# Halving the last row but one between ScalarE and VectorE, and coarser steps in the first two chunks, in a relu row-sum kernel

## The chip, the cores and the metric

The kernel runs on one core of one Trainium2 chip. The metric is the device time of one execution in microseconds (us). Two times appear here. The **time** is what the chip reports for an execution. The **span** is what the profile covers: from the first to the last instruction of the kernel itself. The time is longer, by 1.35 us in the profiled run of the kernel before: it takes in more than the kernel's own instructions.

All runs told of here were with a granted clock of 1.0.

## The reference

```python
# x: 32 x 512 x 1024 float32
relu_x = np.maximum(x, 0)
return np.sum(relu_x, axis=-1).astype(np.float32)
```

There are 16,384 rows of 1024 numbers. On 128 partitions that is 128 rows a partition. 67.1 MB are read and 65 KB are written.

## The kernel before

SyncE issues all transfers on one queue. Seven chunks of 16 rows a partition go through three buffers; then come pieces of 8, 4, 2 and 1 rows, and the last row in three pieces of columns. In the first six chunks ScalarE applies relu to a step of several rows and VectorE sums that step. Later each engine does whole rows alone, with relu and sum in one instruction and an accumulator read of one column (0.19 us on ScalarE, 0.08 on VectorE) after it. The engines and the transfers wait for each other by semaphores: counters that one raises and another waits for.

```python
STEPS = [4, 5, 7]          # rows in each step of chunks 0 to 4
MIXED = [3, 4, 5]          # chunk 5
TAIL = [8, 4, 2, 1]
LAST = [576, 256, 192]     # columns of the pieces of the last row
...
    for c in range(NBIG + 1):
        if c >= NB:
            sp.wait_ge(s_dve, 3 * (c - NB + 1))     # the buffer is free again
        ... sp.dma_start(out=buf[:, c % NB, :, :], ...).then_inc(s_in[c], 16)
...
        for i, n in enumerate(steps):
            t = buf[:, b, r : r + n, :]
            act.activation(t, t, AF.Relu).then_inc(s_act, 1)
            dve.wait_ge(s_act, 3 * c + i + 1)
            dve.tensor_reduce(out=res[...], in_=t, axis=X, op=ALU.add).then_inc(s_dve, 1)
            r += n
...
    for r, n, s in tail:                    # the last of these is row 14, alone
        if n > 1:
            act.wait_ge(s, 16)
        dve.wait_ge(s, 16)
        for i in range(r, r + n):
            f = on_act if (i - r) % 2 else on_dve
            f(buf[:, tb, i, :], res[:, j0 + i : j0 + i + 1])

    n = LAST[2]                             # the last row, in three pieces
    act.wait_ge(s_in[-3], 16)
    on_act(parts[0], last[:, n : n + 1]).then_inc(s_tact, 1)
    dve.wait_ge(s_in[-2], 16)
    on_dve(parts[1], last[:, n + 1 : n + 2]).then_inc(s_tpart, 1)
    dve.wait_ge(s_tpart, 1)
    dve.wait_ge(s_in[-1], 16)
    dve.wait_ge(s_tact, 1)
    on_dve(last[:, :], res[:, J - 1 : J]).then_inc(s_tdve, 1)
```

The sums of the first two pieces are laid behind the third piece, so the last instruction sums 192 numbers and two partial sums.

Of the kernel before, what the change touches and what calls it, by code (L numbers as in the profile page):

```python
# [2 lines left out]

P = 128
D = 1024
BIG = 16
NTWO = 6
NB = 3
REGIONS = [112, 16]
CHUNKS = [(0, 0), (0, 16), (0, 32), (0, 48), (0, 64), (0, 80), (0, 96)]  # L10
STEPS = [4, 5, 7]
MIXED = [3, 4, 5]
TAIL = [8, 4, 2, 1]
LAST = [576, 256, 192]


def bass_relu_sum_kernel(
    nc: bass.Bass,
    x: bass.AP,
    out: bass.AP,  # L20
):







    fp32 = mybir.dt.float32
    ALU = mybir.AluOpType  # L30
    AF = mybir.ActivationFunctionType
    X = mybir.AxisListType.X

    B, S, _ = x.shape
    J = B * S // P
    NBIG = len(CHUNKS)
    assert BIG * NBIG + sum(TAIL) + 1 == J == sum(REGIONS) and sum(LAST) == D

    xr = x.rearrange("b s d -> (b s) d")
    of = out.rearrange("b s -> (b s)")  # L40
    start = [sum(REGIONS[:i]) for i in range(len(REGIONS))]
    xv = [
        xr[P * s : P * (s + n), :].rearrange("(p j) d -> p j d", p=P)
        for s, n in zip(start, REGIONS)
    ]
    ov = [of[P * s : P * (s + n)].rearrange("(p j) -> p j", p=P) for s, n in zip(start, REGIONS)]

    buf = nc.alloc_sbuf_tensor("buf", [P, NB, BIG, D], fp32)
    last = nc.alloc_sbuf_tensor("last", [P, LAST[2] + 2], fp32)
    res = nc.alloc_sbuf_tensor("res", [P, J], fp32)  # L50

    n_in = NBIG + len(TAIL) + len(LAST)
    s_in = [nc.alloc_semaphore(f"s_in{i}") for i in range(n_in)]
    s_act = nc.alloc_semaphore("s_act")
    s_dve = nc.alloc_semaphore("s_dve")
    s_fact = nc.alloc_semaphore("s_fact")
    s_fdve = nc.alloc_semaphore("s_fdve")
    s_tact = nc.alloc_semaphore("s_tact")
    s_tpart = nc.alloc_semaphore("s_tpart")
    s_tdve = nc.alloc_semaphore("s_tdve")  # L60
    s_store = nc.alloc_semaphore("s_store")
    s_out = nc.alloc_semaphore("s_out")

    sp, act, dve = nc.sync, nc.scalar, nc.vector


    tb = NBIG % NB


    code = nc.main_func.blocks[0].instructions  # L70
    arrival = next(
        i
        for i, ins in enumerate(code)
        if ins.engine == mybir.EngineType.SP and type(ins).__name__ == "InstDrain"
    )
    for c in range(NBIG + 1):
        if c >= NB:
            sp.wait_ge(s_dve, 3 * (c - NB + 1))
        if c < NBIG:
            g, j = CHUNKS[c]  # L80
            sp.dma_start(out=buf[:, c % NB, :, :], in_=xv[g][:, j : j + BIG, :]).then_inc(
                s_in[c], 16
            )
        if c == 0:
            code.insert(arrival, code.pop())
    r = 0
    tail = []
    for i, n in enumerate(TAIL):
        sp.dma_start(out=buf[:, tb, r : r + n, :], in_=xv[-1][:, r : r + n, :]).then_inc(  # L89
            s_in[NBIG + i], 16  # L90
        )
        tail.append((r, n, s_in[NBIG + i]))
        r += n
    n0, n1 = LAST[0], LAST[0] + LAST[1]
    parts = [buf[:, tb, r, 0:n0], buf[:, tb, r, n0:n1], last[:, 0 : LAST[2]]]
    for k, (lo, hi) in enumerate([(0, n0), (n0, n1), (n1, D)]):
        sp.dma_start(out=parts[k], in_=xv[-1][:, BIG - 1, lo:hi]).then_inc(
            s_in[NBIG + len(TAIL) + k], 16
        )
    sp.wait_ge(s_fact, 1)  # L100
    sp.wait_ge(s_fdve, 1)
    for g in range(len(REGIONS) - 1):
        sp.dma_start(
            out=ov[g][:, :], in_=res[:, start[g] : start[g] + REGIONS[g]]
        ).then_inc(s_store, 16)


    def on_act(t, acc):
        return act.activation(t, t, AF.Relu, accum_out=acc)  # L109

    def on_dve(t, acc):
        return dve.tensor_scalar(  # L112
            out=t, in0=t, scalar1=0.0, scalar2=None, op0=ALU.max, op1=ALU.add, accum_out=acc
        )

    def row(c, i):
        return buf[:, c % NB, i, :], res[:, c * BIG + i : c * BIG + i + 1]

    for c in range(NTWO):
        b, steps = c % NB, STEPS if c < NTWO - 1 else MIXED  # L120
        act.wait_ge(s_in[c], 16)
        if steps is MIXED:
            dve.wait_ge(s_in[c], 16)
            for i in (BIG - 4, BIG - 3):
                on_dve(*row(c, i))
        r = 0
        for i, n in enumerate(steps):
            t = buf[:, b, r : r + n, :]
            act.activation(t, t, AF.Relu).then_inc(s_act, 1)  # L129
            dve.wait_ge(s_act, 3 * c + i + 1)  # L130
            dve.tensor_reduce(  # L131
                out=res[:, c * BIG + r : c * BIG + r + n], in_=t, axis=X, op=ALU.add
            ).then_inc(s_dve, 1)
            r += n
        if steps is MIXED:
            for i in (BIG - 2, BIG - 1):
                on_act(*row(c, i))


    j0 = NBIG * BIG  # L140
    for c in range(NTWO, NBIG):
        act.wait_ge(s_in[c], 16)
        dve.wait_ge(s_in[c], 16)
        for i in range(BIG):
            ins = (on_act if i % 2 else on_dve)(*row(c, i))
            if i >= BIG - 2:
                ins.then_inc(s_fact if i % 2 else s_fdve, 1)
    for r, n, s in tail:
        if n > 1:
            act.wait_ge(s, 16)  # L150
        dve.wait_ge(s, 16)
        for i in range(r, r + n):
            f = on_act if (i - r) % 2 else on_dve
            f(buf[:, tb, i, :], res[:, j0 + i : j0 + i + 1])

    n = LAST[2]
    act.wait_ge(s_in[-3], 16)
    on_act(parts[0], last[:, n : n + 1]).then_inc(s_tact, 1)
    dve.wait_ge(s_in[-2], 16)
    on_dve(parts[1], last[:, n + 1 : n + 2]).then_inc(s_tpart, 1)  # L160
    dve.wait_ge(s_tpart, 1)
    dve.wait_ge(s_in[-1], 16)
    dve.wait_ge(s_tact, 1)  # L163
    on_dve(last[:, :], res[:, J - 1 : J]).then_inc(s_tdve, 1)


    sp.wait_ge(s_tdve, 1)
    sp.dma_start(out=ov[-1][:, :], in_=res[:, start[-1] : J]).then_inc(s_out, 16)
    sp.wait_ge(s_store, 16 * (len(REGIONS) - 1))
    sp.wait_ge(s_out, 16)  # L170


# [1 line left out]
_INS = ['x']  # L174
_OUTS = [((32, 512), 'float32')]


# [21 lines left out]
```

## Time and profile before

| | before |
|---|---|
| time, median of the first three runs | 161.3 us (161.19 to 161.36) |
| span of the profiled run | 159.9 us |
| load queue q1, share of 16 engines | 97.9% |
| arrival of row 14 to the issue of the last store | 2.09 us |

The page of the kernel before. Lines with an engine's name give busy time, share of the span and number of instructions; lines with a queue's name give packets, MB and share of 16 engines' span; the last is the chain of waits by engine.

```profile
span 159.9 us, 148 instructions
...
DVE 122.0 (76%) x58; ACT 101.0 (63%) x55; POOL 0.2 (0%) x4
...
DMA packets 2305, 67.18 MB, mean 420 GB/s; under 512 B 512, under 2 KB 768, under 8 KB 1024
...
q1 hardware_dynamic: 2304, 67.18, 97.9%
q14 instruction: 1, 0.01, 0.0%
...
DMA 69%; ACT 18%; DVE 11%; SPq 1%; issue 0%; DVEq 0%
```

The load queue is busy for 97.9% of the span, and 69% of the chain is DMA. The q14 line is one packet of 8 KB that is not data, but instructions.

The tail of the kernel before, from the timeline (start in us, duration in us, engine, line, operation, out<-in, shapes):

```profile
156.32 1.22 DVE L112 TENSOR_SCALAR_CACHE_REDUCE buf<-buf 128x1024 f32<-128x1024 f32 x1
157.08 0.68 ACT L109 ACTIVATE buf<-buf 128x576 f32<-128x576 f32 x1 [0.90 <-DMA buf<-in_x_dram]
157.47 0.08 DVE L112 DVE_READ_ACCUMULATOR buf<-buf 128x1 f32 x1
157.47 0.41 DVE L112 TENSOR_SCALAR_CACHE_REDUCE buf<-buf 128x256 f32<-128x256 f32 x1
157.67 0.19 ACT L109 ACTIVATION_READ_ACCUMULATOR buf<-buf 128x1 f32 x1
...
158.02 0.36 DVE L112 TENSOR_SCALAR_CACHE_REDUCE last<-last 128x194 f32<-128x194 f32 x1
...
158.41 0.34 SPq L168 DMA_DIRECT2D out_dram<-res  x1
```

Row 14 keeps VectorE from 156.32 on, and only at 157.47 come the 256 columns, and the last sum starts at 158.02. The store is issued at 158.41, which is 2.09 us after VectorE began row 14. From issue to landing it took (out<-in, KB, median us to landing, in the view of DMA issues):

```profile
out_dram<-res SPq DMA_DIRECT2D x1, 8.0 KB, 1.4
```

### The profile page before, as it was taken

The page shows a single profiled execution, that of the slowest core. Times are in us where ns is not written, and L with a number is a line of the kernel's source. Part 1 is how long each engine was busy: PE and PEld are TensorE (multiplying, and loading weights), DVE is VectorE, ACT ScalarE, POOL GpSimd, SP SyncE. Part 2 cuts the span into 40 slices and gives each one's busy share as a digit, 9 for nine tenths or more (in the row PEclk, how much of TensorE's full clock was granted, in tenths as well). Part 3 has the DMA queues.
Part 4 walks back from the last instruction along what each step waited for, and adds up shares of the span by engine and source line. Part 5 has one row for each costly group of instructions (what it writes and reads, how often), then busy time and mean ns, then how long its engine had stood idle before and what let it go on. Part 6 is the DMA issues. An engine that isn't in the chain of part 4 may idle for free.

```text
span 159.9 us, 148 instructions
## 1 busy us (share of the span) xinstructions
DVE 122.0 (76%) x58; ACT 101.0 (63%) x55; POOL 0.2 (0%) x4
## 2 busy tenths in 40 slices
DVE  0000006989879897998969989699899999598995
ACT  3000059990699808996099941999339980496972
POOL 0000000000000000000000000000000000000000
DMA  7996996996996997989979969969969969899993
GB/s 262 525 525 262 525 525 262 525 525 262 525 492 295 525 459 328 525 377 410 525 312 476 525 262 525 525 262 525 525 262 525 525 262 525 385 402 394 414 407 116
DMA packets 2305, 67.18 MB, mean 420 GB/s; under 512 B 512, under 2 KB 768, under 8 KB 1024
## 3 DMA queue, kind: packets, MB, share of 16 engines
q1 hardware_dynamic: 2304, 67.18, 97.9%
q14 instruction: 1, 0.01, 0.0%
HBM read 67.11 MB, written 0.07 MB: 420 GB/s over the span
## 4 chain that ended last, share of the span: by engine, by line
DMA 69%; ACT 18%; DVE 11%; SPq 1%; issue 0%; DVEq 0%
DMA buf<-in_x_dram 69%; ACT buf L129 18%; DVE res L131 10%; DVE buf L112 1%; SPq L89 1%; DVE last L112 0%; DVEq L163 0%
## 5 line engine op out<-in xcount | busy, mean ns | idle before, releaser
L131 DVE TENSOR_REDUCE res<-buf 128x4 f32<-128x4096 f32 (+3 forms) x18 | 100.4, 5604 | 33.6 <-ACT buf L129 33.6
L129 ACT ACTIVATE buf<-buf 128x4096 f32<-128x4096 f32 (+3 forms) x18 | 80.8, 4553 | 46.3 <-DMA buf<-in_x_dram 46.3
L109 ACT ACTIVATE buf<-buf 128x1024 f32<-128x1024 f32 (+1 forms) x18 | 18.4, 1024 | 9.8 <-DMA buf<-in_x_dram 9.8
L112 DVE TENSOR_SCALAR_CACHE_REDUCE buf<-buf 128x1024 f32<-128x1024 f32 (+1 forms) x19 | 21.3, 1173 | 2.7 <-DMA buf<-in_x_dram 2.5
L109 ACT ACTIVATION_READ_ACCUMULATOR buf<-buf 128x1 f32 x18 | 3.4, 186 | 0.0
L129 ACT ACT_TABLE_LOAD x1 | 1.3, 1283 | 0.8 <-PEq L184 0.8
L112 DVE DVE_READ_ACCUMULATOR buf<-buf 128x1 f32 x19 | 1.6, 83 | 0.0
L112 DVE TENSOR_SCALAR_CACHE_REDUCE last<-last 128x194 f32<-128x194 f32 x1 | 0.4, 356 | 0.1
L184 POOL MEMSET const-bfloat16-1.0<- 128x1 bf16 x1 | 0.1, 102 | 0.0
L184 POOL MEMSET const-uint8-127<- 128x1 uint8 x1 | 0.1, 102 | 0.0
L184 POOL MEMSET const-float32-0.0<- 128x1 f32 x1 | 0.1, 100 | 0.2 <-issue 0.2
L184 POOL MEMSET const-float32-1.0<- 128x1 f32 x1 | 0.1, 99 | 0.0
L112 DVE DVE_READ_ACCUMULATOR last<-last 128x1 f32 x1 | 0.1, 83 | 0.0
## 6 DMA issues: line engine op xcount, KB each, us to landing
buf<-in_x_dram SPq DMA_DIRECT2D x1, 4096.0 KB, 26.7
buf<-in_x_dram SPq DMA_DIRECT2D x1, 2048.0 KB, 31.2
buf<-in_x_dram SPq DMA_DIRECT2D x1, 1024.0 KB, 33.2
buf<-in_x_dram SPq DMA_DIRECT2D x1, 512.0 KB, 34.0
buf<-in_x_dram SPq DMA_DIRECT2D x1, 288.0 KB, 34.3
buf<-in_x_dram SPq DMA_DIRECT2D x1, 128.0 KB, 34.1
buf<-in_x_dram SPq DMA_DIRECT2D x7, 36.3
last<-in_x_dram SPq DMA_DIRECT2D x1, 96.0 KB, 33.9
```

Source lines behind the costliest of these rows:

```text
L89: sp.dma_start(out=buf[:, tb, r : r + n, :], in_=xv[-1][:, r : r + n, :]).then_inc(s_in[NBIG + i], 16)
L109: return act.activation(t, t, AF.Relu, accum_out=acc)
L112: return dve.tensor_scalar(out=t, in0=t, scalar1=0.0, scalar2=None, op0=ALU.max, op1=ALU.add, accum_out=acc)
L129: act.activation(t, t, AF.Relu).then_inc(s_act, 1)
L131: dve.tensor_reduce(out=res[:, c * BIG + r : c * BIG + r + n], in_=t, axis=X, op=ALU.add).then_inc(s_dve, 1)
L184: nc = _bacc.Bacc("TRN2", target_bir_lowering=False, num_devices=1)
```

## The change

The intent is to take VectorE's work on row 14 out of the way of the last row. ScalarE and VectorE each take half of row 14 and a tiny addition joins the sums; the pieces of the last row become 512, 256 and 256 columns; one semaphore counts the two partial sums. In the first two chunks the steps become 7 and 9 rows. The core of the diff:

```diff
-STEPS = [4, 5, 7]
-MIXED = [3, 4, 5]
+STEPS = [[7, 9], [7, 9], [4, 5, 7], [4, 5, 7], [4, 5, 7], [3, 4, 5]]
-LAST = [576, 256, 192]
+LAST = [512, 256, 256]
...
-            sp.wait_ge(s_dve, 3 * (c - NB + 1))
+            sp.wait_ge(s_dve, done[c - NB])
...
-    for r, n, s in tail:
-        if n > 1:
-            act.wait_ge(s, 16)
+    for r, n, s in tail[:-1]:
+        act.wait_ge(s, 16)
...
+    r, _, s = tail[-1]
+    act.wait_ge(s, 16)
+    dve.wait_ge(s, 16)
+    on_act(buf[:, tb, r, 0 : D // 2], half[:, 0:1]).then_inc(s_half, 1)
+    on_dve(buf[:, tb, r, D // 2 : D], half[:, 1:2]).then_inc(s_half, 1)
+    dve.wait_ge(s_half, 2)
+    dve.tensor_tensor(
+        out=res[:, j0 + r : j0 + r + 1], in0=half[:, 0:1], in1=half[:, 1:2], op=ALU.add
+    )
...
-    on_act(parts[0], last[:, n : n + 1]).then_inc(s_tact, 1)
+    on_act(parts[0], last[:, n : n + 1]).then_inc(s_part, 1)
-    on_dve(parts[1], last[:, n + 1 : n + 2]).then_inc(s_tpart, 1)
-    dve.wait_ge(s_tpart, 1)
+    on_dve(parts[1], last[:, n + 1 : n + 2]).then_inc(s_part, 1)
+    dve.wait_ge(s_part, 2)
     dve.wait_ge(s_in[-1], 16)
-    dve.wait_ge(s_tact, 1)
```

## The prediction

> **What bounds the kernel now.** The load of the input. The DMA section gives queue q1 97.9% of 16 engines' span. The timeline shows the 16-row chunks released every 19.35 us (ScalarE starts at 21.84, 41.19, 60.54): 8.39 MB in 19.35 us is 434 GB/s. [...] In the chain of waits, DMA holds 69%; its ScalarE and VectorE links are buffer releases, long before the queue runs dry. Only the work after the last bytes can be shortened.
>
> **The tail before (timeline, us).** Row 14 lands 156.30. The 576-column piece lands about 157.06, the 256-column piece about 157.4, the 192-column piece about 157.7 (issue time plus time to landing). ScalarE takes the 576 piece from 157.08 to 157.86 with its accumulator read. VectorE takes row 14 alone (1.22 us), so the 256 piece starts at 157.47, not when it lands; it ends at 157.89; 0.13 us later (wait instruction 0.05, issue 0.07) the last sum (0.36 us, 194 columns) runs 158.02 to 158.38. The span ends at 159.9.
>
> **What the change does.** From the trace, a VectorE sum costs 1.217 us for 1024 columns and 0.415 for 256: 1.04 ns a column plus 0.15 fixed. ScalarE: 1.06 for 1024 and 0.684 for 576, so 0.63 for 512, plus a 0.19 accumulator read (0.09 overlapped). [...]
> - Row 14 halved: VectorE needs about 0.68 instead of 1.22, done near 157.0; ScalarE done near 157.05. The tiny add, at about 157.12, I estimate at 0.06 to 0.1 (the accumulator reads of one column take 0.08): done near 157.2.
> - New landings by bytes: 512 piece 156.97, 256 piece 157.32, last 256 piece 157.68 (as before, same bytes in all).
> - ScalarE's 512 piece: 157.0 to 157.75. VectorE's 256 piece: 157.34 to 157.76, started by its landing, not by row 14.
> - The last sum starts near 157.87, 0.15 earlier, but has 258 columns instead of 194, which costs 0.42 instead of 0.36. It ends near 158.30: 0.08 us gained.
>
> The halving wins about 0.15; the larger last piece gives 0.065 back.
>
> **Steps [7, 9] in the first two chunks.** Two instructions fewer on each engine, but VectorE starts later (after 6.2 us for 7 rows instead of 3.6 for 4). Its reduction of chunk 0 ends near 45.6 instead of 43.5, and of chunk 1 near 65 instead of 62.9. The loads of chunks 3 and 4 are issued then; the queue is fed until 60.5 and 79.9. Some 15 us of slack: no effect.
>
> **Prediction.** 161.22 us, range 161.02 to 161.42. The gain (0.05%) is within the spread before (161.19 to 161.36). Faster by over 2%: 0.005; within 2%: 0.985; slower by over 2%: 0.01.
>
> **What would show each step.** Right: q1 still near 98%, chunks still 19.35 us apart; VectorE's row-14 half near 0.68 us; the 256 piece with idle time before it ended by DMA; the last sum of 258 columns near 0.42 us, starting 157.8 to 157.95; last store issue near 158.33 instead of 158.41. Wrong: a gap in the load stream near 60 or 80 us; the tiny add or its wait above 0.25 us, so that the 256 piece starts after 157.45 again; ScalarE's 512 piece ending after 157.85.
>
> **What would make it wrong.** A slower stream (piece sizes of 2048 and 1024 bytes a partition instead of 2304, 1024 and 768), a costlier semaphore handover between the two engines than 0.13 us, or another chip with another stream rate.

The sum came to 161.22 us: the 161.3 of before, less the 0.08 gained in the tail.

## The result and the profile after

| | before | after |
|---|---|---|
| time, median of 6 runs each | 161.35 us (161.19 to 161.56) | 161.78 us (161.71 to 161.95) |
| span of the profiled run | 159.9 us | 159.9 us |
| time minus span, profiled run | 1.35 us | 1.86 us |
| time minus span, mean | 1.35 us (9 later runs) | 1.88 us (6 runs) |

Spans of runs other than the profiled ones are on record to 0.1 us, so a single "time minus span" of theirs is good to 0.05 us.

The ratio is 1.0028 (95% interval 1.0015 to 1.0041). Ratios here are the mean time of one kernel's fast runs over that of the other's of the same rounds, so not quite the ratio of the medians quoted.

The change lost 0.43 us, and the span did not see it. The page after, for the same lines as before:

```profile
span 159.9 us, 147 instructions
...
DVE 121.4 (76%) x57; ACT 101.5 (63%) x55; POOL 0.2 (0%) x4
...
DMA packets 2304, 67.18 MB, mean 420 GB/s; under 512 B 512, under 2 KB 768, under 8 KB 1024
...
q1 hardware_dynamic: 2304, 67.18, 97.9%
...
DMA 68%; ACT 18%; DVE 11%; SPq 1%; issue 0%
```

The queue, the chain and the span are as before. VectorE has 57 instructions in place of 58. There is no q14 line: the packets are 2304 instead of 2305, and no packet of instructions is recorded within the span.

The tail after, from the timeline:

```profile
156.47 0.63 ACT L111 ACTIVATE buf<-buf 128x512 f32<-128x512 f32 x1
156.47 0.69 DVE L114 TENSOR_SCALAR_CACHE_REDUCE buf<-buf 128x512 f32<-128x512 f32 x1
...
157.15 0.63 ACT L111 ACTIVATE buf<-buf 128x512 f32<-128x512 f32 x1
157.22 0.16 DVE L164 TENSOR_TENSOR res<-half 128x1 f32<-128x1 f32 x1
157.52 0.42 DVE L114 TENSOR_SCALAR_CACHE_REDUCE buf<-buf 128x256 f32<-128x256 f32 x1
...
157.98 0.42 DVE L114 TENSOR_SCALAR_CACHE_REDUCE last<-last 128x258 f32<-128x258 f32 x1
...
158.44 0.34 SPq L179 DMA_DIRECT2D out_dram<-res  x1
```

The tail did what it was meant to do. VectorE's half of row 14 takes 0.69 us, the tiny addition 0.16, and the 256-column piece starts, at 157.52, only when it has landed, at 157.49 (the chain of waits leads from DMA to it). From the start of row 14 to the issue of the store it is 158.44 - 156.47 = 1.97 us, against 2.09: 0.12 us won. That this is not in the profiled span is an accident of the load, which in this run arrived 0.14 to 0.18 us later from the first chunk on (row 14 at 156.47 against 156.32; it starts at 156.24 in e5 and at 156.68 in e8). In the records, the last of a load's 16 completions comes about 0.11 us behind the fifteenth there, and at most 0.04 behind it in the run before.

So the loss lies after the kernel's last instruction. The profile's views stop there, but the trace's raw records go on, to 1.46 us before and 2.10 us after: semaphore updates and packets of the instruction queue. After the change each of the semaphores 7 to 255 is updated once there, in five blocks of rising numbers (7 to 53, 54 to 104, 105 to 155, 156 to 206, 207 to 255) that run largely at the same time. Semaphore 2 is updated in two rounds, from 0.12 to 0.28 us and again from 1.10 us on. The records give an update's semaphore and time, not its purpose: reading the blocks as a clearing of the semaphores, and the two rounds as a barrier before and after it, is the author's. Both are called so here, and an update of semaphore 2 a hop. The records, us from the span's end:

```
                                            before           after
barrier before the clearing, last hop       0.28             0.28
block  54 to 104: first, last clear         0.35, 0.60       0.34, 0.57
block 105 to 155: first, last clear         0.34, 0.64       0.34, 0.61
block 156 to 206: first, last clear         0.30, 0.62       0.85, 1.14
block   7 to  53: first, last clear         0.50, 0.84       0.49, 0.83
barrier after the clearing, fourth hop      1.22             1.31
barrier after the clearing, last hop        1.46             1.55
instruction packets of 8192 bytes, start    -0.19            +1.33, +1.64
end of the last of them                     +0.15            +2.10
```

Exactly one block starts 0.55 us late. Exactly one instruction packet, which before was fetched 0.19 us ahead of the span's end, is not fetched there any more. But the barrier that follows is through only 0.09 us later, so the late block alone is not the 0.5 us. What is later by more than that are the packets: after the change two are fetched while the barrier closes and just after it, and the last of them ends at 2.10. The table of all runs comes back to this.

### The profile page after: what moved, and what is told of

It is laid out like the page before. It is cut to its first block, busy times and chain, and to the rows that moved or that the text cites. A ratio compares the mean times of both kernels' runs of the same rounds, so it can differ in the third digit from the quotient of the medians.

```text
span 159.9 us, 147 instructions
## 1 busy us (share of the span) xinstructions
DVE 121.4 (76%) x57; ACT 101.5 (63%) x55; POOL 0.2 (0%) x4
## 2 busy tenths in 40 slices
DMA packets 2304, 67.18 MB, mean 420 GB/s; under 512 B 512, under 2 KB 768, under 8 KB 1024
## 3 DMA queue, kind: packets, MB, share of 16 engines
q1 hardware_dynamic: 2304, 67.18, 97.9%
## 4 chain that ended last, share of the span: by engine, by line
DMA 68%; ACT 18%; DVE 11%; SPq 1%; issue 0%
DMA buf<-in_x_dram 68%; ACT buf L132 18%; DVE res L135 11%; SPq L91 1%; SPq L99 0%; DVE buf L114 0%; DVE last L114 0%
## 5 line engine op out<-in xcount | busy, mean ns | idle before, releaser
L135 DVE TENSOR_REDUCE res<-buf 128x7 f32<-128x7168 f32 (+4 forms) x16 | 100.1, 6284 | 34.1 <-ACT buf L132 34.1
L132 ACT ACTIVATE buf<-buf 128x7168 f32<-128x7168 f32 (+4 forms) x16 | 80.7, 5099 | 46.6 <-DMA buf<-in_x_dram 46.6
L111 ACT ACTIVATE buf<-buf 128x1024 f32<-128x1024 f32 (+1 forms) x19 | 19.0, 1000 | 9.0 <-DMA buf<-in_x_dram 8.9
L114 DVE TENSOR_SCALAR_CACHE_REDUCE buf<-buf 128x1024 f32<-128x1024 f32 (+2 forms) x19 | 20.9, 1146 | 2.8 <-DMA buf<-in_x_dram 2.5
```

The lines of the kernel that those rows point to most:

```text
L111: return act.activation(t, t, AF.Relu, accum_out=acc)
L114: return dve.tensor_scalar(out=t, in0=t, scalar1=0.0, scalar2=None, op0=ALU.max, op1=ALU.add, accum_out=acc)
L135: dve.tensor_reduce(out=res[:, c * BIG + r : c * BIG + r + n], in_=t, axis=X, op=ALU.add).then_inc(s_dve, 1)
```

## The experiments

The theory before these runs, **A**: the number of an engine's instructions decides when its last packet of instructions is fetched. With one VectorE instruction fewer, that packet comes only after the kernel's end, and VectorE must wait for it when it should clear its semaphores. The two traces show a packet that is gone from -0.19 us and a block that starts 0.55 us late; that the count moves the one, and that VectorE waits in the other, was the guess for the runs to test. The rivals: **B**, the steps of 7 and 9 rows cost the time; **C**, the new tail does; **D**, the sizes of the last pieces do.

Counts below are those of the trace. VectorE has 61 before and 60 after (the page's 58 and 57, and three more that it does not count as busy: a drain and two waits); ScalarE has 57 in both. "This" and "before" ran in the same rounds, five of "this" each.

### e1: the change with the old steps

```diff
-STEPS = [[7, 9], [7, 9], [4, 5, 7], [4, 5, 7], [4, 5, 7], [3, 4, 5]]
+STEPS = [[4, 5, 7], [4, 5, 7], [4, 5, 7], [4, 5, 7], [4, 5, 7], [3, 4, 5]]
```

> The changed kernel, but the first two chunks in steps of 4, 5, 7 rows again (two instructions more on VectorE and on ScalarE). The span of after (159.9) was that of before, while its time was 0.45 us longer, so 0.5 us lie outside the span: time minus span is 1.33 before and 1.82 to 1.94 after. Theory A (the count of instructions shifts where the instruction stream is fetched, and after the kernel an engine waits for its next instructions): the time can go either way, but time minus span moves in a step of about 0.5, with the traffic of the instruction queue near the end. Theory B (the steps of 7 and 9 rows cost the time): 161.25, 0.1 below before. Theory C (the new tail costs the time, by the tiny add or the order of its waits): 161.8 as in after.

161.33 us, before 161.38; ratio 1.0001 (0.9988 to 1.0013). The loss is gone with the old steps, which B expects too and C does not: C has fallen. But time minus span is 1.49 in the mean, not 1.35, and another block of semaphores (54 to 104) starts late, at 0.67 instead of 0.34. Theory B has no reason for that. A's step "of about 0.5" did not come either: the mean lies between its two values.

### e2: before with the new steps

```diff
-STEPS = [4, 5, 7]
-MIXED = [3, 4, 5]
+STEPS = [[7, 9], [7, 9], [4, 5, 7], [4, 5, 7], [4, 5, 7], [3, 4, 5]]
 (and the loops and counts for it, as in the change)
```

> The kernel before with only the steps of 7 and 9 rows in the first two chunks (two instructions fewer on each of the two engines). Theory B: 161.8, all of the loss. Theory C: 161.35 as before. Theory A: span 159.9 as before; time minus span either 1.3 or 1.85, whatever the tail does.

161.61 us, before 161.38; ratio 1.0022 (1.0008 to 1.0036). Time minus span is 1.70, with block 156 to 206 late (0.72). Neither fits well: A had expected 1.3 or 1.85, and B the whole loss, 161.8. The next run parts them.

### e3: the change with one idle instruction

```diff
+    dve.memset(pad[:, :], 0.0)        # one column, before VectorE's first work
     k = 0
     for c, steps in enumerate(STEPS):
```

> The changed kernel with one idle instruction more on VectorE at the very start (a memset of one column, 20 us before VectorE has work), so VectorE has as many instructions as before (61 in the trace, ScalarE 57). Theory A: the count of before is back on both engines, so time minus span falls back to about 1.35 and the time to 161.25, or 0.5 below after. Theories B and C: the memset does nothing, 161.8.

161.27 us, before 161.38; ratio 0.9995 (0.9983 to 1.0008). Time minus span is back at 1.38. *Adding* an instruction took half a microsecond off the change. Its DMA view has the instruction packet again:

```profile
core 0 of [0], span 160.0 us
...
DMA packets 2305, 67.18 MB, mean 420 GB/s; under 512 B 512, under 2 KB 768, under 8 KB 1024
...
q1 hardware_dynamic: 2304, 67.18, 97.9%
q14 instruction: 1, 0.01, 0.0%
```

Steps and tail are those of the change, so B and C cannot be the cause.

### e4: the change with the old pieces

```diff
-LAST = [512, 256, 256]
+LAST = [576, 256, 192]
```

> The changed kernel with the last row in pieces of 576, 256, 192 again; all instruction counts as in after. Theory A: 161.8 within 0.15, time minus span still about 1.85. A rival by which the sizes of the last pieces cost the time: 161.3. By the sums inside the span alone I expect it within 0.1 of after.

161.57 us, before 161.38; ratio 1.0023 (1.001 to 1.0037). Still slow, so D falls. A had the direction, but its number was missed: it expected 161.8 within 0.15, and by the span within 0.1 of the change's 161.78. The five values of time minus span fall in two groups, 1.56 and 1.60 against 1.87, 1.90 and 1.92. The profiled run was one of the low ones; what its packets suggest stands below the table of all runs.

### e5: before with one VectorE instruction fewer, and nothing else

```diff
             act.activation(t, t, AF.Relu).then_inc(s_act, 1)
+            r += n
+            if c == 0 and i == 0:
+                continue                      # VectorE sums rows 0 to 8 in one
+            m = STEPS[0] + n if c == 0 and i == 1 else n
 (and the load's wait count less one)
```

> The kernel before with one VectorE instruction fewer and nothing else: in the first chunk ScalarE still works in 4, 5, 7 rows, VectorE sums 9 and 7 (VectorE 60 instructions in the trace, ScalarE 57, as in the changed kernel). Theory A (61 VectorE instructions put the last fetch of its instruction stream before the kernel's end, 60 put the need for it after the end): time minus span rises from 1.35 to 1.7 to 1.9, time 161.75, VectorE's clearing of its semaphores after the span begins some 0.5 us late. Rivals (steps of 7 and 9, the new tail): the old tail and a first load wait that moves by nothing that counts, so 161.35.

161.72 us, before 161.26; ratio 1.0031 (1.0018 to 1.0044). This is the whole loss of the change, made in the old kernel by joining two reductions more than 100 us before the end. Time minus span is 1.85, block 156 to 206 starts at 0.86. Its DMA view has lost the q14 line:

```profile
core 0 of [0], span 159.8 us
...
DMA packets 2304, 67.18 MB, mean 420 GB/s; under 512 B 512, under 2 KB 768, under 8 KB 1024
...
q1 hardware_dynamic: 2304, 67.18, 97.9%
```

And its tail is untouched:

```profile
156.24 1.22 DVE L112 TENSOR_SCALAR_CACHE_REDUCE buf<-buf 128x1024 f32<-128x1024 f32 x1
...
157.95 0.35 DVE L112 TENSOR_SCALAR_CACHE_REDUCE last<-last 128x194 f32<-128x194 f32 x1
...
158.34 0.34 SPq L171 DMA_DIRECT2D out_dram<-res  x1
```

2.10 us from row 14 to the store, as before (2.09).

### e6: four idle instructions, in the middle

```diff
     for c, steps in enumerate(STEPS):
+        if c == 4:
+            for i in range(4):
+                dve.memset(pad[:, i : i + 1], 0.0)
```

> The changed kernel with four idle VectorE memsets of one column before chunk 4 instead of one at the start (VectorE 64, ScalarE 57). Theory A: what counts is how many instructions there are, not where they stand, so fast again: time minus span 1.35, time 161.25. If the memset of the earlier run helped because it stood at the start (a warm-up of VectorE), this stays at 161.75.

161.8 us, before 161.26; ratio 1.0039 (1.0027 to 1.0052). This missed in the time, though not in the place: time minus span is 1.36 as A expects, but the *span* grew to 160.4 to 160.7. The store was issued at 158.51 and took 1.9 us to land instead of 1.4. In the records, 15 of its 16 completions had come by 159.96 and the last came at 160.40; the instruction packet now went at 159.05, ahead of the store's own packets (159.35 to 159.59). The fetch had moved earlier and, it seemed, into the way of the store. e11 tests it.

### e7 and e8: ScalarE's count

e7 is the change with one idle VectorE memset and ScalarE's first step cut in three (61 and 59); e8 has steps of 7 and 9 rows only in the first chunk (61 and 58).

```diff
e7
+    dve.memset(pad[:, :], 0.0)
-            act.activation(t, t, AF.Relu).then_inc(s_act, 1)
-            k += 1
+            for lo, hi in [(0, 2), (2, 4), (4, n)] if k == 0 else [(0, n)]:
+                u = t[:, lo:hi, :]
+                act.activation(u, u, AF.Relu).then_inc(s_act, 1)
+                k += 1
e8
-STEPS = [[7, 9], [7, 9], [4, 5, 7], ...
+STEPS = [[7, 9], [4, 5, 7], [4, 5, 7], ...
```

> The changed kernel with one idle VectorE memset and with ScalarE's first step of 7 rows cut in three (VectorE 61, ScalarE 59). In the run with the old steps (62 and 59) time minus span was 1.49 in the mean and one block of semaphores (54 to 104) was cleared 0.2 us late. If that was ScalarE's count of 59, this has time minus span near 1.5 and the same late block; if it was VectorE's 62, this has 1.35.

161.56 us, before 161.26; ratio 1.0016 (1.0002 to 1.0029). Time minus span 1.55, block 54 to 104 late (0.65, against 0.35 before; in e1 it was 0.33 late by its first clear, not the 0.2 of the expectation), block 156 to 206 on time (0.31). So ScalarE's count works the same way, on another block.

> The changed kernel with only the first chunk in 7 and 9 rows (VectorE 61, ScalarE 58), nothing idle added. Theory A: VectorE's 61 makes it fast, time minus span 1.35 to 1.5 depending on ScalarE's 58, time 161.25 to 161.4. The theory of the steps of 7 and 9 rows expects half of the loss, 161.55.

161.6 us, before 161.26; ratio 1.0018 (1.0006 to 1.0031). By its median alone, this is what theory B expected and a miss for A. But it is no middle value: time minus span was 1.40 and 1.44 in two runs and 1.90, 1.93 and 1.94 in three. The profiled run was one of the low ones; it shows an instruction packet 0.08 us after the span's end and one late hop in the closing barrier. So 58 on ScalarE seems to be a bad count too, in some executions; what makes the high ones, no profile caught. B is refuted by e3, e9 and e10, which have steps of 7 and 9 rows in both chunks and are fast.

### e9: VectorE's count restored by real work

```diff
-            dve.tensor_reduce(... in_=t ...).then_inc(s_dve, 1)
-            r += n
+            for m in [4, 5] if c == 0 and n == 9 else [n]:
+                dve.tensor_reduce(... in_=buf[:, c % NB, r : r + m, :] ...).then_inc(s_dve, 1)
+                r += m
 (and the loads' wait counts one more)
```

> The changed kernel with VectorE's count of 61 restored by real work: in the first chunk ScalarE keeps 7 and 9 rows, VectorE sums 7, 4 and 5 (VectorE 61, ScalarE 57, nothing idle). Theory A: time minus span 1.35, no late block of semaphores, time 161.2 to 161.3, at or just below before. If only an idle memset helps: 161.75.

161.13 us, before 161.33; ratio 0.9982 (0.9969 to 0.9996). This is the one version that beat both kernels: the change, with one VectorE reduction cut in two. The lead is thin. The kernel before had a mean span of 160.04 in these rounds, against 159.98 and 159.90 in others, and e3 and e10, with the same tail and a good count, gave intervals that include 1. Time minus span is 1.37, and the instruction packet is in the span again:

```profile
core 0 of [0], span 159.9 us
...
DMA packets 2305, 67.18 MB, mean 420 GB/s; under 512 B 512, under 2 KB 768, under 8 KB 1024
...
q1 hardware_dynamic: 2304, 67.18, 97.8%
q14 instruction: 1, 0.01, 0.0%
```

### e10 to e12: moving the fetch

```diff
+    for i in range(2):                 # e10; 3 in e11, 12 in e12
+        dve.memset(pad[:, i : i + 1], 0.0)
     k = 0
```

> The changed kernel with two idle memsets at the start (VectorE 62, ScalarE 57). In the run with 62 and 59 the instruction fetch came at 159.45 instead of 159.69, with 64 at 159.05. Theory A: time minus span 1.35; the fetch near 159.45 just misses the packets of the output store (159.2 to 159.5), so span 159.9 and time 161.25.

161.2 us, before 161.33; ratio 0.999 (0.9977 to 1.0002); time minus span 1.35, span 159.88 in the mean, fetch at 159.45. As expected.

> The changed kernel with three idle memsets at the start (VectorE 63, ScalarE 57). Theory A with the collision that the run with 64 suggests (one of the 16 completions of the output store came 0.44 us after the others): the fetch comes between 159.05 and 159.45, in the way of the store, so time minus span 1.35 but a span of 160.2 to 160.6 and a time of 161.6 to 161.9. If the fetch and the store don't collide: span 159.9, time 161.25.

161.87 us, before 161.33; ratio 1.0029 (1.0016 to 1.0041); time minus span 1.36, span 160.5. The collision, as expected, with the memsets at the start as with those of e6 in the middle (span 160.52). The tail and the store's landing:

```profile
156.42 0.63 ACT L112 ACTIVATE buf<-buf 128x512 f32<-128x512 f32 x1
156.42 0.69 DVE L115 TENSOR_SCALAR_CACHE_REDUCE buf<-buf 128x512 f32<-128x512 f32 x1
...
158.38 0.34 SPq L182 DMA_DIRECT2D out_dram<-res  x1
```

```profile
core 0 of [0], span 160.6 us
...
out_dram<-res SPq DMA_DIRECT2D x1, 8.0 KB, 2.2
```

The tail is on time: 1.96 us from row 14 to the store's issue. The store then takes 2.2 us to land, against 1.4. In the records, its first 15 completions lie between 159.65 and 159.82 and the 16th comes at 160.59, 0.77 us later; the packet of instructions went at 159.06, just before the store's.

> The changed kernel with twelve idle memsets at the start (VectorE 72, ScalarE 57): each VectorE sum of one row is two instructions, so 8 more than in the run with 64 move the fetch some 3 to 5 us ahead, into the load. Theory A: time minus span 1.35; the output store is left alone, but one of 16 engines has 0.3 to 0.5 us of fetch in the load stream, so the last landings come up to 0.3 late: span 159.9 to 160.3, time 161.25 to 161.6. If instead the fetch collision of the run with 64 had another cause (the memsets in the middle of the kernel), nothing says why this should differ from 161.25.

161.88 us, before 161.33; ratio 1.0031 (1.0019 to 1.0044); time minus span 1.34, span 160.56 in the mean. The place was right, the size was not: I had expected up to 0.3 us, from 0.3 to 0.5 us for the fetch (the 8 KB packets in the trace of the kernel before take 0.31 to 0.49 us). The last landing first in the change, then in e12 (KB, median us from issue to landing):

```profile
core 0 of [0], span 159.9 us
...
last<-in_x_dram SPq DMA_DIRECT2D x1, 128.0 KB, 33.8
```

```profile
core 0 of [0], span 160.7 us
...
last<-in_x_dram SPq DMA_DIRECT2D x1, 128.0 KB, 34.8
...
out_dram<-res SPq DMA_DIRECT2D x1, 8.0 KB, 1.4
```

The fetch went at 143.5, in the middle of the load. From the transfer then under way on, one of the 16 completions of every transfer comes 0.93 to 1.02 us behind the other fifteen. Before the fetch, in the same run, it was 0.01 to 0.04 behind. The tail follows a microsecond late and the store itself is quick again (1.4):

```profile
157.28 0.63 ACT L112 ACTIVATE buf<-buf 128x512 f32<-128x512 f32 x1
157.28 0.69 DVE L115 TENSOR_SCALAR_CACHE_REDUCE buf<-buf 128x512 f32<-128x512 f32 x1
...
158.74 0.42 DVE L115 TENSOR_SCALAR_CACHE_REDUCE last<-last 128x258 f32<-128x258 f32 x1
...
159.20 0.34 SPq L182 DMA_DIRECT2D out_dram<-res  x1
```

The fetch packet itself took 0.33 us. Why a load's last completion fell back by about three times that is not shown; that it is the engine which also did the fetch is inferred, since the records name no engine.

### All runs in one table

From the raw records of each profiled run: the instruction packet's time and the first clear of two blocks, us from the span's end; and means of time minus span and of the span over all timed runs (before: of e1's rounds).

```
        VectorE ScalarE  8 KB packets       54-104  156-206  time-span  span
before     61      57    -0.19               0.35    0.30      1.35    159.98
after      60      57    +1.33 +1.64         0.34    0.85      1.88    159.93
e5         60      57    +1.31 +1.63         0.34    0.86      1.85    159.90
e4         60      57    +1.33               0.34    0.85      1.77    159.92
e2         59      55    +1.39               0.34    0.72      1.70    159.94
e3         61      57    -0.18               0.34    0.32      1.38    159.86
e9         61      57    -0.21               0.35    0.30      1.37    159.78
e10        62      57    -0.33               0.34    0.31      1.35    159.88
e11        63      57    -1.58               0.34    0.29      1.36    160.50
e6         64      57    -1.39               0.35    0.29      1.36    160.52
e12        72      57    -17.16              0.34    0.30      1.34    160.56
e8         61      58    +0.08               0.34    0.31      1.72    159.82
e7         61      59    -0.21 +1.30         0.65    0.31      1.55    159.96
e1         62      59    -0.32 +1.31         0.67    0.30      1.49    159.84
```

Read it by VectorE's count, at 57 on ScalarE. At 60 the clearing starts late, and packets are fetched that end after the barrier. At 61 and 62 the packet goes in a gap, after the store's packets and before the closing barrier, and time minus span stays at 1.35 to 1.38. At 63 and 64 it meets the store, at 72 the load. With more instructions the fetch came earlier: at 159.69, 159.45, 159.06, 159.05 and 143.5 us of the span with 61 (before), 62, 63, 64 and 72. Which block of semaphores is late goes with the engine whose count was changed: 156 to 206 with VectorE (0.72 to 0.86 against 0.29 to 0.32), 54 to 104 with ScalarE (0.65 and 0.67 against 0.34 and 0.35). That the engine waits there for a packet of instructions is inferred, since no record shows what it waits for, and the packet that should end that wait was not recorded (records can be missing: of the semaphores 7 to 255, all updated in the trace after, 20 have no update in the one before).

Nor is it this wait that costs most. The same records, set beside the time minus span of the same execution:

```
               barrier's last hop   end of last 8 KB packet   time minus span
after                1.55                  2.10                    1.86
e5                   1.55                  2.08                    1.84
e4                   1.55                  1.84                    1.62
e2                   1.46                  1.90                    1.68
e7                   1.46                  1.82                    1.58
e1                   1.46                  1.80                    1.57
e8                   1.52                  0.39                    1.40
the other 7      1.46 to 1.47          0.17 or earlier         1.35 to 1.36
```

In the six executions with a packet that ends after the barrier, time minus span is 0.22 to 0.24 us less than that packet's end. In the other eight it is 0.11 to 0.12 less than the barrier's last hop. So the loss goes with the fetch that ends last: in e1, e2 and e7 a block is cleared late, yet the barrier is not, and the time is still 0.2 to 0.3 us longer; in the change the barrier is only 0.09 later. One late packet goes with 1.57 to 1.68, two with 1.84 and 1.86, which would fit the two groups of e4; its high runs were not profiled. This is a relation over fourteen traces, found afterwards, and no run tested it. What these late packets hold, and why there are one or two, is open.

## Why the prediction was wrong

- **The bound.** Right. The load queue stayed at 97.9% and the chain at 68% DMA.
- **The tail.** Right, with its sign and nearly its size. 0.08 us were forecast and 0.12 measured from row 14 to the store (2.09 to 1.97). VectorE's half took 0.69 us (0.68 forecast), the last sum 0.42 (0.42). The tiny addition was mis-sized: 0.16 instead of 0.06 to 0.1, an estimate from another kind of instruction (the accumulator read). It cost nothing, since it ended at 157.38 and the next piece landed at 157.49.
- **The span.** Not contradicted: 159.93 in the mean after, 159.90 to 160.04 before; the scatter between rounds is larger than the 0.08 forecast.
- **The step that failed** is the paragraph on the steps of 7 and 9 rows. It noted "Two instructions fewer on each engine" and closed with "no effect", because it looked only for a late load. Buffers and loads were indeed not affected (the load queue at 97.9% before and after). But with the addition of the tail, the net count of VectorE is one fewer, and that alone costs 0.46 us (e5: 161.72 against 161.26). Beneath it lay a term that the forecast treated as a constant without saying so: the 1.4 us between span and time. It measured 1.35 before and 1.88 after. In the profiled runs, the last packet of instructions ended 2.10 us after the span instead of 0.15, with the closing barrier through at 1.55 instead of 1.46.
- The packet that tells it was on the page before the change (q14, one packet), and the prediction did not ask what it was for.

## What to carry to other kernels

When the time moves and the span does not, look past the kernel's last instruction: compare time minus span, the instruction queue's line, and the records after the span: the clearing of semaphores, the closing barrier and above all the packets of instructions that end after it. Read the megabytes of the queue's line too: e4's page has one q14 packet, but of 0.00 MB. In this kernel, the mere number of instructions on an engine was worth half a microsecond (0.46 us in e5), so a comparison of two versions of a few tenths must hold the counts equal, or sweep them by adding idle instructions. Once a good count is found, keep it with useful work (here one reduction cut in two), and check that the instruction fetch falls neither into the load nor onto the output store (in e12 and e11 the span was 0.68 and 0.62 us longer than in e10, same rounds).
